# One-bank PSUM tiles in rotation for the up-projection, two weight blocks loaded into other buffers, and a last product added onto sums kept in PSUM

## The chip, the core and the metric

The kernel runs on one core of one Trainium2 chip. The metric is the device time of one execution in microseconds (us), the median of three runs. A core has five engines that run at the same time and meet only through semaphores: TensorE (PE) for matmuls, with its weight loads shown apart as PEld; VectorE (DVE) and ScalarE (ACT) for element-wise work; GpSimd (POOL), used here for tiny operations and a few DMA issues; and SyncE (SP), whose queue issues nearly all DMAs in order. Matmuls write to PSUM, which has 8 banks of 512 fp32 columns each; everything else lives in SBUF.

## The reference

The block mixes 1024 tokens of width 1024, normalises, applies a gated MLP with a causal convolution, and normalises again. What matters here is the second half:

```python
h = layer_norm(ALPHA * h + mix, ln1_g, ln1_b)
u = h @ w_up                                   # 1024 -> 2 x 2816
uc = conv_b + sum(conv_w[j] * pad(u)[:, j:j + T] for j in range(3))
a, v = split(uc, 2)
h = layer_norm(ALPHA * h + (gelu(a) * v) @ w_down, ln2_g, ln2_b)
```

## The kernel before

Every fp32 product is made of three matmuls (`mm3`, lines 83 to 86): each operand is split into a high part `wh` (ACT, line 66) and a low part `wl` (DVE, line 67), and high-high, high-low and low-high are summed in PSUM. One matmul has 128 x 128 weights and 512 moving columns. The order of instructions within each engine's queue is made by a scheduler when the kernel is built: it follows the order of the code where it can and takes later work forward where an instruction would have to wait. A wait at run time therefore stops its engine, and what stands behind it in that queue.

**Up-projection (lines 655 to 687 and 760 to 761).** A seven-product scheme (instead of eight) on 512 x 512 blocks computes, for each of 22 steps `f`, one gate tile and one value tile. `pair(f)` runs seven products of 12 matmuls each (84 in all) into four accumulators c1 to c4. In order: "11" into c1, "12" into c2, "s2" onto c1, "s1" into c3, "s3" onto c1, "s4" onto c3, "22" into c4. Between them ACT and DVE read the accumulators out: line 665 (c1), 669 (c2), 672 (c1), 677 (c3), 680 (c1), 684 (c3), 687 (c4). c1 and c2 are the two halves of one two-bank tile `u`, c3 and c4 of another; the pool `psp` has four such tiles (`unit()`, line 55). Beside it `post(f-1)` runs convolution, GELU and gate (lines 691 to 731), stores the gated blocks to DRAM (`gd`, line 700), and `prep(f+1)` splits the next weights. The weight `s1` of steps from 2 on sits in the pool `lnp` under the tags "g" and "b" in turn (line 640).

**Down-projection (lines 766 to 986).** Again seven products, P1 to P7, each over six blocks `q` of the inner dimension (`plan`, 42 blocks, n = 0 to 41). For each block `load_a` fetches the gated data (line 776) into one of three `rawp` buffers, `prepare` splits data and weight, and `multiply` runs them into four one-bank accumulators per product (`banks`, pool `pb`, opened when `psp` is closed, line 861). A block is 24 matmuls (4 accumulators x 2 inner tiles x 3), the sixth of each product half of that. Splits go into `wp` buffers or, for the operands numbered 5 to 7 modulo 8, into the pool `dn` (tags dh and dl), which is laid over space that the up-projection has given up. The weights of P1's first four blocks come by `load_b` (line 782): blocks 0 and 1 into `rawp`, blocks 2 and 3 into the `tmp` tiles of pool `zq`, which lie over space given up as well. The other weights are loaded in halves by `load_w2` (line 886), two after each `prepare`. The rows of the first norm's scale and offset are loaded into the tags "g" and "b" (line 878, through line 459) before the down-projection starts.

`finish` adds a product's accumulators to the result tiles `z` (lines 910 and 913). P1, P6, P7 and P4 use the first four banks, P2, P5 and P3 the other four. Tiles z[4..7] get in their low half first `ALPHA * b1 - c` after P7, then the scaled residual (`residual`, line 893), then P4's sums (line 913); then their second statistics (line 488) and the norm (lines 470 to 485). In P4 the first two accumulators run through all blocks, then the third, then the fourth, each followed by its `finish` and norm.

Of the kernel before, what the change touches and what calls it, by code (L numbers as in the profile page):

```python
# [9 lines left out]
F32 = mybir.dt.float32  # L10
# [4 lines left out]
ALU = mybir.AluOpType  # L15
AX = mybir.AxisListType

P = 128
T = 1024
D = 1024  # L20
# [7 lines left out]
ALPHA = 2.0 ** 0.25  # L28
# [14 lines left out]
def block_kernel(ctx: ExitStack, tc: tile.TileContext, x, xT, w_ct, w_i, pool_w, w_out, w_up, w_down, pk, rows, masks, ident, out):  # L43
# [11 lines left out]
    def unit():  # L55
        return ps.tile([P, 1024], F32, tag="u", name="u")
# [398 lines left out]
    z = {}  # L455

    def row(i, tag):
        r = lnp.tile([P, D], F32, tag=tag, name=f"row{i}")
        nc.sync.dma_start(out=r, in_=rows[i:i + 1, :].broadcast_to([P, D]))
        return r  # L460
# [4 lines left out]
        G.tensor_tensor(out=rs, in0=rs, in1=epst[:, 0:1], op=ALU.pow)  # L465
        return rs

    def layer_norm(zt, gam, bet, st6, how, sink):
        mv = small.tile([P, 2], F32, tag="mv", name="mv")
        V.bn_aggr(out=mv, in_=st6.rearrange("p a b -> p (a b)"))  # L470
        rs = rstd(mv)
        if how == "added":
            V.scalar_tensor_tensor(out=zt, in0=zt, scalar=mv[:, 0:1], in1=gam, op0=ALU.subtract, op1=ALU.mult)
            A.activation(out=zt, in_=zt, func=AF.Identity, scale=rs)
            G.dma_start(out=zt, in_=rows[3:4, :].broadcast_to([P, D]), accum_op=ALU.add)
            nc.sync.dma_start(out=sink, in_=zt)
            return
        parts = halves if how == "halves" else [slice(0, D)]
        for c in parts:
            V.scalar_tensor_tensor(out=zt[:, c], in0=zt[:, c], scalar=mv[:, 0:1], in1=gam[:, c], op0=ALU.subtract, op1=ALU.mult)  # L480
        if how == "halves":
            parts = [halves[0], slice(512, 768), slice(768, 1024)]
        for c in parts:
            V.scalar_tensor_tensor(out=zt[:, c], in0=zt[:, c], scalar=rs, in1=bet[:, c], op0=ALU.mult, op1=ALU.add)
            nc.sync.dma_start(out=sink[:, c], in_=zt[:, c])

    def stats(zt, c, st6):
        V.bn_stats(out=st6[:, c.start // 512, :], in_=zt[:, c])
# [163 lines left out]
    B11, T1, B21, B22 = block(0, 0), block(0, 1), block(1, 0), block(1, 1)  # L652
    T2, T3, T4 = [[e[:, i] for e in (th, tlo)] for i in range(3)]

    def pair(f):
        w = ops[f]
        u = unit()
        c1, c2 = u[:, lo], u[:, hi]
        prod(c1, w["11"], B11, True, False)
        if f == BRIDGE:  # L660
            yield
            prod(c2, w["12"], B21, True, True)
            yield
        a, v = outs[f] = [ua.tile([P, T], F32, tag=f"u{n}", name=f"u{n}") for n in "av"]
        A.activation(out=a[:, lo], in_=c1, func=AF.Copy)  # L665
        if f != BRIDGE:
            yield
            prod(c2, w["12"], B21, True, True)
        V.tensor_tensor(out=a[:, lo], in0=c2, in1=a[:, lo], op=ALU.add)
        yield  # L670
        prod(c1, w["s2"], T2, False, False)
        A.activation(out=a[:, hi], in_=c1, func=AF.Copy)
        yield
        u = unit()
        c3, c4 = u[:, lo], u[:, hi]
        prod(c3, w["s1"], T1, True, False)
        A.activation(out=v[:, hi], in_=c3, func=AF.Copy)
        yield
        prod(c1, w["s3"], T3, False, True)
        A.activation(out=v[:, lo], in_=c1, func=AF.Copy)  # L680
        V.scalar_tensor_tensor(out=v[:, hi], in0=v[:, hi], scalar=-1.0, in1=v[:, lo], op0=ALU.mult, op1=ALU.subtract)
        yield
        prod(c3, w["s4"], B22, False, True)
        V.tensor_tensor(out=a[:, hi], in0=c3, in1=a[:, hi], op=ALU.add)  # L684
        yield
        prod(c4, w["22"], T4, True, True)
        V.tensor_tensor(out=v[:, lo], in0=c4, in1=v[:, lo], op=ALU.subtract)  # L687
# [46 lines left out]
    def step(gens, n=1):  # L734
        for i in range(n):
            for g in gens:
                next(g, None)
# [21 lines left out]
    step([preps[2]])  # L759
    for f in range(2, NF - 1):  # L760
        step([pairs[2] if f == 2 else pair(f), post(f - 1), preps[f + 1]], 7)

# [15 lines left out]
    raw_b = {}  # L780

    def load_b(q):
        r = rawp.tile([P, 2, 512], F32, tag="raw", name="rawb") if q < 2 else tmp_tile("rawb").rearrange("p (a t) -> p a t", t=512)
        raw_b[q] = r[:, :len(jps[q])]
        nc.sync.dma_start(out=raw_b[q], in_=w_view(0, q, lo))

# [50 lines left out]
    def first_operands():  # L837
        load_a(0)
        load_b(0)
        yield  # L840
        yield
        yield
        prepare(0)
        yield
        load_a(1)
        load_b(1)
        yield
        yield
        load_a(2)
# [5 lines left out]
    tpp.__exit__(None, None, None)  # L855
    bigp.__exit__(None, None, None)
    uap.__exit__(None, None, None)
    psp.__exit__(None, None, None)
    dn = ctx.enter_context(tc.tile_pool(name="dn", bufs=3, reuse_waits="tile"))
    zq = ctx.enter_context(tc.tile_pool(name="zq", bufs=1, reuse_waits="tile"))  # L860
    pb = ctx.enter_context(tc.tile_pool(name="pb", bufs=1, space=bass.MemoryType.PSUM))
    place = {}

    def w_tile(r_, q):
# [2 lines left out]
    def tmp_tile(name):  # L867
        return zq.tile([P, D], F32, tag="tmp", name=name, bufs=3)
# [6 lines left out]
    for q in range(4, NS):  # L875
        w_tile(1, q)
    ww = [[place[r_, q] for q in range(NS)] for r_ in range(2)]
    g1, b1_ = row(0, "g"), row(1, "b")
    st6 = maskt[:, 0, :NC * 48].bitcast(F32).rearrange("p (t a b) -> p t a b", a=2, b=6)

    w_loads = [(0, q, lo) for q in range(FREE, NS)] + [(1, q, lo) for q in range(2)] + [(0, q, c) for q in range(2) for c in (lo, hi)]
# [7 lines left out]
    def residual(t):  # L889
        zn = tmp_tile("zn")  # L890
        nc.sync.dma_start(out=zn, in_=zd[t])
        V.scalar_tensor_tensor(out=zn, in0=zn, scalar=ALPHA, in1=g1, op0=ALU.mult, op1=ALU.mult)
        V.tensor_tensor(out=z[t], in0=z[t], in1=zn, op=ALU.add)

    banks = {i: [pb.tile([P, 512], F32, name=f"c{i}{p}") for p in range(4)] for i in (1, 3)}
    fresh = {P1: 1, P2: 3, P5: 3, P4: 1}
    where = {P1: 1, P6: 1, P7: 1, P4: 1, P2: 3, P5: 3, P3: 3}

    def multiply(n, ps_):
# [6 lines left out]
                mm3(o, ah[:, jj, ts], al[:, jj, ts], wh[:, jj], wl[:, jj], i in fresh and q == 0 and jj == 0,  # L906
                    q == NS - 1 and jj == len(jps[q]) - 1, skip_group_check=True)

    def first_touch(t, c, src, op):
        V.scalar_tensor_tensor(out=z[t][:, c], in0=b1_[:, c], scalar=ALPHA, in1=src, op0=ALU.mult, op1=op)  # L910

    def more(t, c, src, op):
        V.tensor_tensor(out=z[t][:, c], in0=z[t][:, c], in1=src, op=op)

    def finish(i, p):
        c = banks[where[i]][p]
        if i == P1:
            first_touch(p, lo, c, ALU.add)
        elif i == P2:
            more(p, lo, c, ALU.add)  # L920
        elif i == P6:
            first_touch(p, hi, c, ALU.add)
        elif i == P5:
            first_touch(4 + p, hi, c, ALU.subtract)
        elif i == P7:
            more(4 + p, hi, c, ALU.subtract)
            first_touch(4 + p, lo, c, ALU.subtract)
        elif i == P3:
            more(p, hi, c, ALU.add)
        else:  # L930
            more(4 + p, lo, c, ALU.add)

    def norm2(t, c, how):
        stats(z[t], c, st6[:, t])
        layer_norm(z[t], g2, b2, st6[:, t], how, out[t * P:(t + 1) * P, :])


    beside = []
    prepared = 1
    load_b(2)  # L940
    load_b(3)

    def advance(n):
        nonlocal prepared
        while prepared <= n and prepared < len(plan):
            if prepared not in raw_a:
                load_a(prepared)
            prepare(prepared)
            prepared += 1
            if prepared < len(plan) and prepared not in raw_a:  # L950
                load_a(prepared)
            load_w2(2)

    for n in range(6 * NS):
        i, q = plan[n]
        advance(n + 1)
        multiply(n, range(4))
        if q == NS - 1:
            for p in range(4):
                finish(i, p)  # L960
            if i == P6:
                beside += [lambda t=t: (residual(t), stats(z[t], lo, st6[:, t])) for t in range(4)]
            elif i == P7:
                beside += [lambda t=t: (residual(t), stats(z[t], hi, st6[:, t])) for t in range(4, 8)]
        elif beside:
            beside.pop(0)()
            if i == P3 and not beside:
                g2, b2 = row(2, "g"), row(3, "b")
    n0 = 6 * NS
    for q in range(NS):  # L970
        advance(n0 + q + 1)
        multiply(n0 + q, (0, 1))
        if q < 4:
            norm2(q, hi, "added")
    for p in range(2):
        finish(P4, p)
    for q in range(NS):
        multiply(n0 + q, (2,))
    for p in range(2):
        norm2(4 + p, lo, "whole")  # L980
    finish(P4, 2)
    for q in range(NS):
        multiply(n0 + q, (3,))
    norm2(6, lo, "whole")
    finish(P4, 3)
    norm2(7, lo, "halves")


def _consts():
# [60 lines left out]
```

## Time and profile before

| | us |
|---|---|
| median of 3 runs | 1044.73 (1043.55 to 1045.59) |
| the profiled execution | 1043.8 |
| its span in the trace | 1041.9 |
| PE busy | 1022.6 (98%) |
| DVE busy | 814.6 (78%) |
| ACT busy | 446.1 (43%) |

The page gives each engine's busy time as a share of the span and cuts the span into 40 slices of 26 us. A busy PE counts a matmul from start to modelled end (0.39 us), though the next one starts 0.23 us after it, so short waits between matmuls don't lower the busy share: they are to be looked for in the distance between starts and in the waits of the weight loads. The trace answers with a timeline (start, duration, engine, line, operation, output <- inputs, and in brackets the idle time before and who ended it), with waits by who was waited for, and with busy times for stretches.

### The profile page before, as it was taken

The page shows a single profiled execution, that of the slowest core. Times are in us where ns is not written, and L with a number is a line of the kernel's source. Part 1 is how long each engine was busy: PE and PEld are TensorE (multiplying, and loading weights), DVE is VectorE, ACT ScalarE, POOL GpSimd, SP SyncE. Part 2 cuts the span into 40 slices and gives each one's busy share as a digit, 9 for nine tenths or more (in the row PEclk, how much of TensorE's full clock was granted, in tenths as well). Part 3 has the DMA queues.
Part 4 walks back from the last instruction along what each step waited for, and adds up shares of the span by engine and source line. Part 5 has one row for each costly group of instructions (what it writes and reads, how often), then busy time and mean ns, then how long its engine had stood idle before and what let it go on. Part 6 is the DMA issues. An engine that isn't in the chain of part 4 may idle for free.

```text
span 1041.9 us, 12036 instructions
## 1 busy us (share of the span) xinstructions
PE 1022.6 (98%) x4680; PEld 837.6 (80%) x4680; DVE 814.6 (78%) x975; ACT 446.1 (43%) x562; POOL 49.2 (5%) x77
## 2 busy tenths in 40 slices
PE   9999999999999999999999999999999799999996
PEld 6888888888888887878887787787787588888885
DVE  6495488977754779989788888888886669996786
ACT  6421353323631566644444444444454344334340
POOL 2000000001100100000000000000000100000024
PEclk9999999999999999999999999999999999999999
DMA  8200201100142222314314314313315595553347
GB/s 328 91 21 1 81 22 60 41 1 2 60 182 100 99 85 81 112 71 147 105 51 139 115 54 137 113 59 133 112 60 189 200 391 210 172 171 100 122 114 220
DMA packets 42569, 118.63 MB, mean 114 GB/s; under 512 B 4432, under 2 KB 5328, under 8 KB 42512
## 3 DMA queue, kind: packets, MB, share of 16 engines
q1 hardware_dynamic: 41232, 113.86, 31.2%
q0 software_dynamic: 1136, 3.93, 1.5%
q8 instruction: 37, 0.61, 0.2%
q14 instruction: 20, 0.16, 0.0%
q10 hardware_dynamic: 144, 0.07, 0.0%
HBM read 89.27 MB, written 28.57 MB: 113 GB/s over the span
## 4 chain that ended last, share of the span: by engine, by line
PE 96%; DVE 1%; DMA 1%; ACT 0%; issue 0%; SPq 0%; POOLq 0%; POOL 0%; DVEq 0%; ACTq 0%
PE u L84 24%; PE u L86 23%; PE u L85 23%; PE c L85 6%; PE c L84 6%; PE c L86 6%; PE u L229 3%; PE u L269 1%; PE u L530 1%; DMA rawb<-in_w_down 1%; PE u L271 1%; PE u L258 1%; DMA hg<-in_xT 1%; PE u L196 0%; PE u L197 0%
## 5 line engine op out<-in xcount | busy, mean ns | idle before, releaser
L84 PE MATMUL u<-bh,wh 128*128 128x512 f32 x520 | 203.6, 395 | 1.3 <-ACT ua L665 0.7
L85 PE MATMUL u<-bl,wh 128*128 128x512 f32 x520 | 202.8, 390 | 1.0 <-DVE bl L67 1.0
L86 PE MATMUL u<-bh,wl 128*128 128x512 f32 x520 | 202.5, 390 | 0.0
L67 DVE TENSOR_TENSOR wl<-raw,wh 128x1024 fp32r<-128x1024 f32 x85 | 103.4, 1221 | 26.4 <-ACT wh L66 24.0
L66 ACT ACTIVATE wh<-raw 128x1024 fp32r<-128x1024 f32 x85 | 88.9, 1058 | 77.8 <-PE u L85 63.9
L84 PEld LDWEIGHTS u<-bh,wh 128*128 128x128 f32 x520 | 97.6, 188 | 25.2 <-ACT ua L665 3.3
L85 PEld LDWEIGHTS u<-bl,wh 128*128 128x128 f32 x520 | 97.7, 188 | 21.2 <-DVE bl L67 1.6
L86 PEld LDWEIGHTS u<-bh,wl 128*128 128x128 f32 x520 | 97.6, 188 | 21.0
L84 PE MATMUL u<-th,wh 128*128 128x512 f32 x264 | 106.6, 404 | 0.8 <-DVE ua L684 0.8
L86 PE MATMUL u<-th,wl 128*128 128x512 f32 x264 | 103.4, 392 | 0.0
L85 PE MATMUL u<-tlo,wh 128*128 128x512 f32 x264 | 103.1, 391 | 0.0
L84 PEld LDWEIGHTS u<-th,wh 128*128 128x128 f32 x264 | 49.5, 187 | 21.1 <-DVE ua L684 6.9
L66 ACT ACTIVATE wh<-rawa 128x1024 fp32r<-128x1024 f32 (+1 forms) x30 | 30.1, 1002 | 75.0 <-PE c L85 46.5
L86 PEld LDWEIGHTS u<-th,wl 128*128 128x128 f32 x264 | 49.6, 188 | 11.5 <-DVE wl L67 0.3
L693 DVE SCALAR_TENSOR_TENSOR cv<-uv,pkt,cv 128x1023 f32<-128x1023 f32 (+1 forms) x44 | 56.3, 1280 | 2.7 <-ACT cv L691 2.4
L84 PE MATMUL u<-wh,bh 128*128 128x512 f32 x144 | 57.8, 401 | 0.0
L84 PE MATMUL c<-wh 128*128 128x512 f32 x144 | 56.1, 390 | 1.6 <-DVE uv L687 1.6
L85 PEld LDWEIGHTS u<-tlo,wh 128*128 128x128 f32 x264 | 49.6, 188 | 9.1
L693 DVE SCALAR_TENSOR_TENSOR ca<-ua,pkt,ca 128x1023 f32<-128x1023 f32 (+1 forms) x44 | 56.2, 1278 | 0.2
L86 PE MATMUL u<-wh,bl 128*128 128x512 f32 x144 | 56.2, 390 | 0.0
L85 PE MATMUL u<-wl,bh 128*128 128x512 f32 x144 | 56.1, 390 | 0.0
L85 PE MATMUL c<-wl,wh 128*128 128x512 f32 x144 | 56.0, 389 | 0.0
(229 smaller groups left out, 1977.0 us busy)
## 6 DMA issues: line engine op xcount, KB each, us to landing
raw<-in_w_up SPq DMA_DIRECT2D x42, 512.0 KB, 3.5
w<-in_w_down SPq DMA_DIRECT2D x20, 512.0 KB, 10.4
rawa<-gds SPq DMA_DIRECT2D x20, 512.0 KB, 3.5
gd<-ca SPq DMA_DIRECT2D x30, 256.0 KB, 2.9
rawa<-gd SPq DMA_DIRECT2D x15, 512.0 KB, 4.2
raw<-in_w_ct SPq DMA_DIRECT2D x13, 512.0 KB, 3.3
gds<-sm SPq DMA_DIRECT2D x20, 256.0 KB, 2.4
gds<-ca SPq DMA_DIRECT2D x20, 256.0 KB, 4.0
```

The costliest lines, as they stand in the source:

```text
L66: A.activation(out=h, in_=r, func=AF.Copy)
L67: V.tensor_tensor(out=l, in0=r, in1=h.bitcast(F32), op=ALU.subtract)
L84: PE.matmul(o, lhsT=ah, rhs=bh, start=start, stop=False, **kw)
L85: PE.matmul(o, lhsT=ah, rhs=bl, start=False, stop=False, **kw)
L86: PE.matmul(o, lhsT=al, rhs=bh, start=False, stop=stop, **kw)
L229: PE.matmul(ul[:, p * P:(p + 1) * P], lhsT=km[:, p * P:(p + 1) * P], rhs=view(QF, p * P + hh, [2 * hh, 64 // hh], [512 - hh, 2], [1, hh]), ...
L258: PE.matmul(up[:, c * P:(c + 1) * P], lhsT=KTr[:, c * P:(c + 1) * P], rhs=vchunk(c, hs), start=True, stop=True)
L269: PE.matmul(uo[:, cs], lhsT=vchunk(c, hs), rhs=sc[:, cs], start=True, stop=c == 0)
L271: PE.matmul(uo[:, cs], lhsT=S[:, (c - 1) * P:c * P], rhs=QF[:, cs], start=False, stop=True)
L530: PE.transpose(out=ut[:, k * P:(k + 1) * P], in_=z[t][:, k * P:(k + 1) * P], identity=identt)
L693: V.scalar_tensor_tensor(out=c[:, 2 - j:], in0=u[:, :T - 2 + j], scalar=pkt[:, cw + j:cw + j + 1], in1=c[:, 2 - j:], op0=ALU.mult, op1=ALU ...
```

## The change

- `pair` takes its accumulators from `two()`: from step 3 on, two tiles of one bank each from a pool `pb` of eight one-bank buffers in rotation, opened after step 2 when `psp` is closed. The down-projection's eight accumulators are the next eight tiles of the same rotation.
- `load_b` puts weight blocks 2 and 3 into the tags "g" and "b" of `lnp` instead of `tmp` tiles, and both loads are issued within `first_operands`, beside the last `pair`. The rows of the first norm are loaded into these tags later, at n = 3.
- For z[4..7] the low half is no longer collected in `z`. After P7 `ALPHA * b1 - c` is written back into the bank, the residual is added there, and P4's matmuls add onto it. Statistics and the norm's first operation read the bank; P4's four additions are gone. The norm's first operation runs on two halves, the high one first.

```diff
-    def layer_norm(zt, gam, bet, st6, how, sink):
+    def layer_norm(zt, src, gam, bet, st6, how, sink):
...
-        parts = halves if how == "halves" else [slice(0, D)]
-        for c in parts:
-            V.scalar_tensor_tensor(out=zt[:, c], in0=zt[:, c], scalar=mv[:, 0:1], in1=gam[:, c], op0=ALU.subtract, op1=ALU.mult)
-        if how == "halves":
-            parts = [halves[0], slice(512, 768), slice(768, 1024)]
+        for o, c in zip(src, halves[::-1]):
+            V.scalar_tensor_tensor(out=zt[:, c], in0=o, scalar=mv[:, 0:1], in1=gam[:, c], op0=ALU.subtract, op1=ALU.mult)
+        parts = [halves[1], slice(0, 256), slice(256, 512)] if how == "halves" else [whole]
...
+    def two():
+        if f_banks:
+            return [f_banks[0].tile([P, 512], F32, tag="c", name="c") for i in range(2)]
+        u = unit()
+        return u[:, lo], u[:, hi]
...
-        u = unit()
-        c1, c2 = u[:, lo], u[:, hi]
+        c1, c2 = two()
...
-        u = unit()
-        c3, c4 = u[:, lo], u[:, hi]
+        c3, c4 = two()
...
         step([pairs[2] if f == 2 else pair(f), post(f - 1), preps[f + 1]], 7)
+        if f == 2:
+            psp.__exit__(None, None, None)
+            f_banks.append(ctx.enter_context(tc.tile_pool(name="pb", bufs=8, space=bass.MemoryType.PSUM, reuse_waits="tile")))
...
-        r = rawp.tile([P, 2, 512], F32, tag="raw", name="rawb") if q < 2 else tmp_tile("rawb").rearrange("p (a t) -> p a t", t=512)
+        r = (rawp if q < 2 else lnp).tile([P, 2, 512], F32, tag=("raw", "raw", "g", "b")[q], name="rawb")
...
         load_b(0)
+        load_b(2)
...
         load_b(1)
+        load_b(3)
...
-    psp.__exit__(None, None, None)
-    pb = ctx.enter_context(tc.tile_pool(name="pb", bufs=1, space=bass.MemoryType.PSUM))
...
-    g1, b1_ = row(0, "g"), row(1, "b")
...
-        V.tensor_tensor(out=z[t], in0=z[t], in1=zn, op=ALU.add)
+        if t < 4:
+            V.tensor_tensor(out=z[t], in0=z[t], in1=zn, op=ALU.add)
+            return
+        for o, c in ((z[t][:, hi], hi), (banks[1][t - 4], lo)):
+            V.tensor_tensor(out=o, in0=o, in1=zn[:, c], op=ALU.add)
...
-    banks = {i: [pb.tile([P, 512], F32, name=f"c{i}{p}") for p in range(4)] for i in (1, 3)}
-    fresh = {P1: 1, P2: 3, P5: 3, P4: 1}
+    banks = {i: two() + two() for i in (1, 3)}
+    fresh = {P1, P2, P5}
...
-            first_touch(4 + p, lo, c, ALU.subtract)
+            first_touch(4 + p, lo, c, ALU.subtract, c)
...
+            c = banks[1][t - 4]
+            V.bn_stats(out=st6[:, t, 0, :], in_=c)
+            src = [z[t][:, hi], c]
...
-    load_b(2)
-    load_b(3)
...
+        if n == FREE - 1:
+            g1, b1_ = row(0, "g"), row(1, "b")
...
-    for p in range(2):
-        finish(P4, p)
-    for q in range(NS):
-        multiply(n0 + q, (2,))
-    for p in range(2):
-        norm2(4 + p, lo, "whole")
-    finish(P4, 2)
-    for q in range(NS):
-        multiply(n0 + q, (3,))
-    norm2(6, lo, "whole")
-    finish(P4, 3)
-    norm2(7, lo, "halves")
+    for p in range(2, 4):
+        for q in range(NS):
+            multiply(n0 + q, (p,))
+        if p == 2:
+            for t in range(2):
+                norm2(4 + t, "whole")
+    norm2(6, "whole")
+    norm2(7, "halves")
```

## Rows read from the trace of the kernel before

**Rows 1.** The page: the span, and PE's busy tenths in 40 slices.
```profile
span 1041.9 us, 12036 instructions
...
PE   9999999999999999999999999999999799999996
```

**Rows 2.** Stretches (from:to, length, busy us and count of each engine, granted clock, DMA).
```profile
446.53:549.33 102.80, 102.80 (x446) 82.26 (x445) 88.25 (x103) 50.30 (x60) 0.00 (x0) 1.00 0.26 92
549.33:782.67 233.34, 233.34 (x1009) 186.01 (x1009) 197.28 (x229) 109.78 (x132) 0.00 (x0) 1.00 0.30 102
782.67:813.79 31.12, 30.33 (x129) 23.48 (x128) 20.48 (x22) 12.22 (x15) 0.81 (x1) 1.00 0.51 172
...
1014.57:1032.93 18.36, 18.36 (x82) 15.21 (x81) 14.14 (x19) 2.31 (x2) 10.54 (x12) 1.00 0.97 278
```

**Rows 3.** Waits of PE's weight loads, 500 to 809 (us in total, times, longest).
```profile
PEld u L84 <- DVE ua L684: 4.8, 16, 0.3
PEld u L84 <- ACT ua L672: 3.4, 16, 0.4
PEld u L84 <- ACT ua L665: 1.6, 8, 0.2
PEld u L84 <- ACT uv L677: 1.4, 7, 0.2
PEld u L84 <- DVE ua L669: 1.2, 7, 0.2
```

**Rows 4.** Timeline of the last pair: ACT, PE, DVE, PE.
```profile
803.68 0.60 ACT L672 ACTIVATE ua<-u 128x512 f32<-128x512 f32 x1 [3.13 <-PE u L86]
...
809.72 0.39 PE L86 MATMUL u<-bh,wl 128*128 128x512 f32 x1
...
810.14 0.69 DVE L684 TENSOR_TENSOR ua<-u,ua 128x512 f32<-128x512 f32 x1 [1.40 <-PE u L86]
...
810.89 0.50 PE L84 MATMUL u<-th,wh 128*128 128x512 f32 x1 [0.79 <-DVE ua L684]
```

**Rows 5.** Timeline of PE from the last pair to the down-projection's first block.
```profile
813.56 0.39 PE L86 MATMUL u<-th,wl 128*128 128x512 f32 x1
815.50 0.47 PE L84 MATMUL c<-wh 128*128 128x512 f32 x1 [1.55 <-DVE uv L687]
```

**Rows 6.** Timeline before the third block (n = 2): PE, SP's queue, ACT, PE.
```profile
826.26 0.39 PE L86 MATMUL c<-wh,wl 128*128 128x512 f32 x1
...
823.92 0.45 SPq L785 DMA_DIRECT2D rawb<-in_w_down  x1
...
830.64 1.06 ACT L66 ACTIVATE dh<-rawb 128x1024 fp32r<-128x1024 f32 x1 [8.56 <-DMA rawb<-in_w_down]
...
831.75 1.22 PE L84 MATMUL c<-dh,wh 128*128 128x512 f32 x2 [5.10 <-ACT dh L66]
```

**Rows 7.** The third block as a stretch (columns as in rows 2).
```profile
831.75:840.04 8.29, 8.25 (x25) 6.16 (x25) 5.99 (x6) 4.08 (x6) 0.00 (x0) 0.68 1.05 391
```

**Rows 8.** Timeline of SP's queue: the loads into the tags "g" and "b".
```profile
782.00 0.33 SPq L459 DMA_DIRECT2D row<-in_rows  x1
...
804.36 0.33 SPq L459 DMA_DIRECT2D row<-in_rows  x1
```

**Rows 9.** Timeline of DVE: the last post's end, and the third block's low part.
```profile
823.44 0.68 DVE L731 TENSOR_TENSOR ca<-sm,ca 128x512 f32<-128x512 f32 x1
831.73 1.23 DVE L67 TENSOR_TENSOR dl<-rawb,dh 128x1024 fp32r<-128x1024 f32 x1 [7.60 <-ACT dh L66]
```

**Rows 10.** Block n = 7: ACT's split, PE's first matmul, and the stretch around them.
```profile
847.23 1.06 ACT L66 ACTIVATE dh<-rawa 128x1024 fp32r<-128x1024 f32 x1 [5.20 <-DMA rawa<-gd]
...
859.08 0.39 PE L84 MATMUL c<-dh 128*128 128x512 f32 x1
...
845.00:855.00 10.00, 10.00 (x46) 8.26 (x44) 5.16 (x7) 4.02 (x4) 0.00 (x0) 1.00 1.04 394
```

**Rows 11.** Timeline of the end: DVE's addition of P4's last sums.
```profile
1033.36 0.69 DVE L913 TENSOR_TENSOR z<-z,c 128x512 f32<-128x512 f32 x1 [2.08 <-PE c L86]
```

More of the change, by code (lines that the diff above doesn't have):

```diff
@@ L653, in block_kernel @@
     T2, T3, T4 = [[e[:, i] for e in (th, tlo)] for i in range(3)]
+    def two():
[3 more added lines that the diff above has]
+        return u[:, lo], u[:, hi]
+    f_banks = []
     def pair(f):
         w = ops[f]
-        u = unit()
-        c1, c2 = u[:, lo], u[:, hi]
+        c1, c2 = two()
         prod(c1, w["11"], B11, True, False)
@@ L907, in multiply, with first_touch @@
                     q == NS - 1 and jj == len(jps[q]) - 1, skip_group_check=True)
-    def first_touch(t, c, src, op):
-        V.scalar_tensor_tensor(out=z[t][:, c], in0=b1_[:, c], scalar=ALPHA, in1=src, op0=ALU.mult, op1=op)
+    def first_touch(t, c, src, op, o=None):
+        V.scalar_tensor_tensor(out=z[t][:, c] if o is None else o, in0=b1_[:, c], scalar=ALPHA, in1=src, op0=ALU.mult, op1=op)
     def more(t, c, src, op):
@@ L926, in finish, with norm2 @@
             more(4 + p, hi, c, ALU.subtract)
-            first_touch(4 + p, lo, c, ALU.subtract)
+            first_touch(4 + p, lo, c, ALU.subtract, c)
         elif i == P3:
             more(p, hi, c, ALU.add)
-        else:
[L931 to L935, printed above, removed]
+    def norm2(t, how):
+        if t < 4:
+            stats(z[t], hi, st6[:, t])
+            src = z[t]
+        else:
+            c = banks[1][t - 4]
+            V.bn_stats(out=st6[:, t, 0, :], in_=c)
+            src = [z[t][:, hi], c]
+        layer_norm(z[t], src, g2, b2, st6[:, t], how, out[t * P:(t + 1) * P, :])
     beside = []
     prepared = 1
-    load_b(2)
-    load_b(3)
     def advance(n):
@@ L973, in block_kernel @@
         if q < 4:
-            norm2(q, hi, "added")
-    for p in range(2):
-        finish(P4, p)
-    for q in range(NS):
-        multiply(n0 + q, (2,))
-    for p in range(2):
-        norm2(4 + p, lo, "whole")
-    finish(P4, 2)
-    for q in range(NS):
-        multiply(n0 + q, (3,))
-    norm2(6, lo, "whole")
-    finish(P4, 3)
-    norm2(7, lo, "halves")
+            norm2(q, "added")
+    for p in range(2, 4):
[6 more added lines that the diff above has]
+    norm2(7, "halves")
 def _consts():
```

## The prediction

> **What bounds the kernel.** The page comes first: PE is busy in nearly every slice, and only two of the forty show less than nine tenths, the 32nd (807 to 834 us) and the last [rows 1]. So time can be won only where PE waits: in those two slices, and in waits too short for the slices to show. For the short ones I need the ideal pace. Near the end 81 matmul starts take 18.36 us without a wait [rows 2], 0.2267 us each. A pair of the up-projection has 84 matmuls, so 19.04 us. Twelve pairs ran from 549.33 to 782.67, 233.34 us, against 12 x 19.04 = 228.5: 4.8 us lost, 0.40 a pair. The stretch before (446 matmuls, 101.1 us by the pace, 102.80 measured) loses 1.7, the one behind (129 matmuls, 29.2 by the pace, 31.12 measured) 1.9 [rows 2]. Together 8.4 us, some 0.2 us more or less for each record the trace may miss. Third, the waits of the weight loads name the cause, and the timeline shows the three large stops at 810, 814 and 827 us [rows 3 to 6].
>
> **A. One-bank tiles in the pairs.** Of the 54 waits in 500 to 809 us, 31 (L684, L665, L669; 7.6 of 12.4 us) end with a read of the other half of the two-bank tile that PE is about to write: c3 read, c4 wanted; c1 read, c2 wanted; c2 read, c1 wanted [rows 3]. Rows 4 show the largest: "s4" ends, DVE reads c3 for 0.69 us, and only then "22" starts in the other bank, 1.17 us after the matmul before it instead of 0.23. With a tile for each bank this dependency is gone. The other 23 (L672, L677; 4.8 us) are true ones: a product is added onto the bank that ACT has just read. In the code's order 12 matmuls into another accumulator, 12 x 0.2267 = 2.7 us, stand between, and the read takes 0.60 us once ACT gets to it [rows 4]; they are exposed before because parts of "s1" had been taken forward to fill the first kind of wait. Where these fillers are no longer needed, the true waits are covered as well. Bounds: 8.4 x 7.6 / 12.4 = 5.1 us if they stay as they are, 8.4 if all go. I take 7.5, near the upper end, because of the 2.7 against 0.60. The rotation itself costs nothing: a bank comes round again after a whole pair, 19 us after its last matmul, and each is read out within a pair. DVE is busy 197.28 of 233.34 us there [rows 2]; with 12 pairs in 228.5 us it would be at 86%, so it doesn't take over.
>
> **B. The change of stage.** The first block of the down-projection starts 1.94 us after the last pair's last matmul, 1.71 more than the pace; PE waited for L687, the last read of the old pool [rows 5]. The eight accumulators are now the next of the same rotation: 19 pairs (steps 3 to 21) take 76 tiles, so P1's four are the banks of pair 20, long read out, and its operands don't hang on the pool. 1.7 us go, and nothing else is late there; what hides the last read is the first block itself.
>
> **C. The third weight block.** PE stops at 826.26 + 0.23 = 826.49 and goes on at 831.75: 5.3 us [rows 6]. The load was issued at 823.92 on SP's queue and landed 6.7 us later, when ACT started at once. Then the block takes 8.29 us at a granted clock of 0.68 of full speed, against 24 x 0.2267 = 5.4: another 2.85 us [rows 7]. Together 8.1. In the changed kernel blocks 2 and 3 are loaded when "g" and "b" become free. In the trace before, the row loads went into these tags at 782.00 and 804.36 us [rows 8]; so both blocks land some 15 us before they are wanted. What is late next is DVE. Its chain through the last post begins with L684 at 810.14, when "s4" has ended, and runs with hardly a gap to 823.44 + 0.68 = 824.12 [rows 4, 9]; it hangs on "s4", not on PE's waits behind it. PE, without the stops at 810 and 814, would come to block 2 at about 810.0 + 2.7 + 48 x 0.2267 = 823.6. If block 2's low part (1.23 us) stands behind the post on DVE, it is ready at 825.3: 1.7 us are left of the stop. If it is put in front of part of the post: none. If ACT's split can't start before the post has freed its `dn` buffer, which the trace doesn't show: 824.1 + 1.06 + 1.23 = 826.4, 2.8 us. I take the middle, 1.7, because the queue there is full by the rows. A stop of that size before 815.50 left the pace whole (47 starts in the 10.76 us from there to 826.26, 0.229 each [rows 5, 6]), so the 2.85 goes too. C = 8.1 - 1.7 = 6.4, bounds 5.3 and 8.1.
>
> The two row loads that give way (line 878) now stand on SP's queue at n = 3, each behind the split that frees its tag (about 825 and 829). Behind them wait gated data and weights for later blocks. Bytes are the same: two blocks leave the burst, two rows enter it.
>
> **E. What the earlier PE meets.** From 825 us on the DMA queues are full: 394 GB/s at a share of 1.04 from 845 to 855 [rows 10]. The next data to be late is that of block n = 7: ACT got it at 847.23, having waited 5.2 us, so with 1.06 and 1.23 us of splits it is ready at 849.5; PE wanted it at 859.08 [rows 10]. PE comes about 0.9 + 1.7 + 6.4 = 9.0 us earlier after this change: 850.1. So the 9.6 us of cushion are used up, and that is all. If the burst starts as early as before, nothing is lost; for each us that it starts later PE loses one, and 2.85 more should the clock fall. I take 0.5 us lost, bounds 0 and 7 (4 us of stop, the wait for "b", and a fall of the clock).
>
> **D. The end.** After PE's last matmul DVE's addition of 0.69 us stands on the path to the end [rows 11]. It goes. Statistics and the first norm operation now read PSUM. The trace has the same price for both: L913 with one PSUM operand takes 0.69 us, L731 from SBUF alone 0.68 [rows 9, 11]. The four residual additions are split into two of 0.69 each, on a DVE that PE isn't waiting for there, and stand beside P3's first blocks, so P4, which now needs them, finds them done. The two-part norm of tiles 4 to 6 costs DVE about 0.2 us each, inside the 2.08 us that DVE idles before L913 [rows 11]. D = 0.7.
>
> On D the Trainium skill says otherwise: "VectorE: DVE Perf Modes", section "The TRN2 errata — SBUF-src ops pay a fixed extra latency per instruction", gives VectorE a fixed part of 120 cycles from PSUM and 58 from SBUF at 0.96 GHz. By that, two such operations on the last path would cost an estimated 0.13 us more, and D would be 0.6; the rows of this trace show no such difference.
>
> **Sum.** 7.5 + 1.7 + 6.4 + 0.7 - 0.5 = 15.8 us. The profiled execution took 1043.8 us (span 1041.9 and 1.9 around it), which gives 1028.0. The median of the runs is 0.9 above the profiled one, so 1029.
>
> **The rivals.** (1) *The load burst becomes the bound.* For it: the full DMA queues and a cushion of 9.6 us of which 9.0 are used [rows 10]; the row loads wait on the same queue as the burst. Against: two blocks leave the burst, and it waited for no PE. It gives back up to 7 us: 1035 to 1036. (2) *The order of PE's queue leaves waits in the pairs*, at weights or at the true reads: A falls to 3 or so, 1033. For it: 39% of the waits are true ones [rows 3]. (3) *The change doesn't do what it says at block 2*: the load is early, but something else behind the last post frees block 2, or SP's order still puts the loads behind a blocked one. Then C brings nothing: 1035. (4) *Slower: the clock falls in the pairs.* Place: the change from one bank to the next; price: 2.85 us for each fall [rows 7]; it decides from 15.8 / 2.85, six falls in the 19 pairs. One in each pair would give 1029 + 54 = 1083. Against: the granted clock is 1.00 throughout the pairs before, with 54 short waits in it [rows 2, 3], and the change takes waits away.
>
> For rival 4 a page of the Trainium skill speaks: "TensorE: Matmul & The Clock Gate", section "A second HAM failure mode: psum-queue depth-cycling", tells of a kernel that cycled through PSUM banks and whose PE idled briefly between groups so often that the clock swung between its two levels. This trace has cycled through four two-bank tiles with the clock at its higher level, so it doesn't bear that out.
>
> **How the numbers follow.** Forecast, 1024 to 1033: 0.68. Rival 1: 0.13. Rival 2 below what the forecast's range holds: 0.05. Rival 3: 0.05. Rivals 1 and 3 together, or the like, which leaves about no gain: 0.03. Rival 4 and late loads beyond all bounds, slower: 0.06. All gains at their upper ends give 1044.7 - 8.4 - 1.7 - 8.1 - 0.7 = 1025.8; I put the low end at 1024 for records missed in A. All at their lower ends give 1044.7 - 5.1 - 1.7 - 5.3 - 0.6 + 7 = 1039; 8 in 10 are held by 1024 to 1037. About 0.2% (2 us) is what a measurement of this kernel can tell from no change. Faster 0.91, same 0.03, slower 0.06.
>
> **What would show it.** A: the weight loads' waits on L684, L665 and L669 gone, pairs 38.1 us for two instead of 38.9. B: the first c matmul 0.23 us after the last of the pairs. C: `rawb` loaded into the "g" and "b" tiles before 810 us, block 2 started with less than 2 us of stop, granted clock 1.00 around it. E: no PE stop from 840 to 870. D: statistics directly behind the last matmul. Wrong would make it: new waits of PE on weights in the pairs, SP's queue blocked at a row load while the DMA queues run dry, or a granted clock below 1.00 before 800 us.

## The result, and the profile after

The changed kernel takes 1029.66 us (median of 4 runs, 1028.29 to 1031.09) against 1044.33 (4 runs, 1043.55 to 1045.59): a ratio of 0.9859, 95% interval 0.9839 to 0.9878. Forecast were 1029.0 us, range 1024 to 1037. The profiled execution took 1028.29 us with a span of 1026.5, so the spans differ by 1041.9 - 1026.5 = 15.4 us. That is the sum to be explained, against 15.8 forecast.

The page of the kernel after: span, PE's busy tenths in 40 slices and its granted clock.

```profile
span 1026.5 us, 12046 instructions
PE   8999999999999999999999999999999999999997
PEclk9999999999999999999999999999999999999999
```

The weak 32nd slice of before [rows 1] is gone. The slices hide one small stop, which the windows of the kernel after show in the last of three stretches, as 12.42 us busy of 14.00 (us, then busy time and instructions of PE, PEld, DVE, ACT and POOL, granted clock, DMA share, GB/s):

```profile
442.70:800.00 357.30, 357.30 (x1576) 295.43 (x1575) 304.48 (x351) 175.22 (x205) 0.81 (x1) 1.00 0.32 108
800.00:826.00 26.00, 26.00 (x117) 21.52 (x116) 17.30 (x18) 9.80 (x10) 3.24 (x6) 1.00 0.58 180
826.00:840.00 14.00, 12.42 (x54) 9.63 (x53) 9.43 (x11) 5.89 (x7) 0.00 (x0) 1.00 1.05 395
```

The whole list of waits of PE's weight loads from 443 us to 1019 us has two entries, where before had five rows in the pairs alone [rows 3]:

```profile
PEld c L84 <- ACT wh L66: 1.9, 1, 1.9
PEld c L85 <- DVE wl L67: 0.5, 1, 0.5
```

And the timeline of PE at the places where the prediction put its steps (start, duration, engine, line, operation; in brackets idle time and releaser):

```profile
435.38 0.50 PE L84 MATMUL u<-th,wh 128*128 128x512 f32 x1 [0.46 <-ACT ua L677]
...
440.74 0.39 PE L86 MATMUL u<-bh,wl 128*128 128x512 f32 x1
442.01 0.50 PE L84 MATMUL u<-th,wh 128*128 128x512 f32 x1 [0.88 <-DVE ua L688]
...
444.88 0.39 PE L84 MATMUL c<-bh,wh 128*128 128x512 f32 x1
...
806.92 0.39 PE L86 MATMUL c<-th,wl 128*128 128x512 f32 x1
807.15 0.39 PE L84 MATMUL c<-wh 128*128 128x512 f32 x1
...
818.03 0.39 PE L84 MATMUL c<-dh,wh 128*128 128x512 f32 x1
...
828.68 0.39 PE L86 MATMUL c<-dh,dl 128*128 128x512 f32 x1
830.59 1.19 PE L84 MATMUL c<-wh 128*128 128x512 f32 x4 [1.52 <-ACT wh L66]
831.85 0.50 PE L85 MATMUL c<-wl,wh 128*128 128x512 f32 x1
```

From 444.88, where the first one-bank tile is written, to 807.15 the 19 pairs take 362.27 us, which is 1596 matmuls of 0.227: the ideal pace. Two stops are left in the last pair that has two-bank tiles: 0.62 us before 435.38 (L677, L672 before, a true wait) and 1.04 us before 442.01 (the neighbouring half); the second kind stood at 810.89 before [rows 4]. The stage changes within 0.23 us (806.92, 807.15; 1.94 before, [rows 5]). Block 2 starts at 818.03 = 807.15 + 48 x 0.2267 without any stop (5.3 us before, [rows 6]), and the granted clock, 0.68 there before [rows 7], is 1.00. New is the stop at block 4: 828.68 to 830.59, 1.68 us more than the pace, and some 0.5 us behind it where low parts come one by one.

Measured in the two profiled executions: pairs 813.56 - 806.92 = 6.64; stage change 1.71; block 2 with its clock 8.1; block 4 -2.2; the end 1.02. The sum is 15.3.

### The profile page after: what moved, and what is told of

Same layout as the page of the kernel before. It is cut to its first block, busy times and chain, and to the rows that moved or that the text cites. A ratio compares the mean times of both kernels' runs of the same rounds, so it can differ in the third digit from the quotient of the medians.

```text
span 1026.5 us, 12046 instructions
## 1 busy us (share of the span) xinstructions
PE 1012.7 (99%) x4680; PEld 840.6 (82%) x4680; DVE 810.5 (79%) x978; ACT 449.7 (44%) x562; POOL 45.8 (4%) x77
## 4 chain that ended last, share of the span: by engine, by line
PE 92%; DVE 5%; DMA 1%; issue 1%; ACT 1%; SPq 0%; POOL 0%; POOLq 0%; DVEq 0%; ACTq 0%
PE c L85 18%; PE c L86 18%; PE c L84 18%; PE u L84 11%; PE u L85 11%; PE u L86 11%; PE u L229 3%; DVE wl L67 1%; DMA w<-in_w_down 1%; DVE ca L697 1%; DVE cv L697 1%; PE u L269 1%; PE u L528 1%; PE u L271 1%; PE u L258 1%
## 5 line engine op out<-in xcount | busy, mean ns | idle before, releaser
L84 PE MATMUL u<-bh,wh 128*128 128x512 f32 x292 | 115.0, 396 | 1.3 <-ACT ua L670 0.7
L85 PE MATMUL u<-bl,wh 128*128 128x512 f32 x292 | 114.0, 390 | 1.0 <-DVE bl L67 1.0
L86 PE MATMUL u<-bh,wl 128*128 128x512 f32 x292 | 113.8, 390 | 0.0
L84 PE MATMUL c<-bh,wh 128*128 128x512 f32 x228 | 88.7, 389 | 0.0
L85 PE MATMUL c<-bl,wh 128*128 128x512 f32 x228 | 88.7, 389 | 0.0
L86 PE MATMUL c<-bh,wl 128*128 128x512 f32 x228 | 88.7, 389 | 0.0
L84 PE MATMUL c<-th,wh 128*128 128x512 f32 x228 | 88.7, 389 | 0.0
L85 PE MATMUL c<-tlo,wh 128*128 128x512 f32 x228 | 88.7, 389 | 0.0
L86 PE MATMUL c<-th,wl 128*128 128x512 f32 x228 | 88.7, 389 | 0.0
L85 PEld LDWEIGHTS u<-bl,wh 128*128 128x128 f32 x292 | 54.9, 188 | 12.3 <-DVE bl L67 1.6
L697 DVE SCALAR_TENSOR_TENSOR ca<-ua,pkt,ca 128x1023 f32<-128x1023 f32 (+1 forms) x44 | 56.2, 1278 | 0.1
L697 DVE SCALAR_TENSOR_TENSOR cv<-uv,pkt,cv 128x1023 f32<-128x1023 f32 (+1 forms) x44 | 56.2, 1277 | 0.0
```

Of the source, the lines that this page charges most:

```text
L84: PE.matmul(o, lhsT=ah, rhs=bh, start=start, stop=False, **kw)
L85: PE.matmul(o, lhsT=ah, rhs=bl, start=False, stop=False, **kw)
L86: PE.matmul(o, lhsT=al, rhs=bh, start=False, stop=stop, **kw)
L697: V.scalar_tensor_tensor(out=c[:, 2 - j:], in0=u[:, :T - 2 + j], scalar=pkt[:, cw + j:cw + j + 1], in1=c[:, 2 - j:], op0=ALU.mult, op1=ALU ...
```

## The experiments

The times of the runs below stand beside a median of before of 1044.84 us (7 runs, first four experiments) and 1044.31 us (11 runs, last four). The changed kernel ran beside the last four only (1029.27); the first four are set against its 1029.66 above, beside which before took 1044.33, so half a microsecond between them tells nothing.

**Without part 1.** The pairs and the down-projection get their accumulators as before, parts 2 and 3 stay.

```
-        c1, c2 = two()
+        u = unit()
+        c1, c2 = u[:, lo], u[:, hi]
...
-    banks = {i: two() + two() for i in (1, 3)}
+    banks = {i: [pb.tile([P, 512], F32, name=f"c{i}{p}") for p in range(4)] for i in (1, 3)}
```

> The changed kernel with part 1 undone: two-bank tiles in all pairs, the down-projection's accumulators in a pool of their own opened behind the last pair. Theory (the stretch from the last pairs to the fifth block hangs on DVE's chain and on SP's queue behind it, so a gain before it is partly swallowed): the pairs end 6.6 us later and the first down-projection block another 1.7, but weight block 4 lands at a time that hangs on the end of the last 's4' product, so its stop of about 2 us shrinks to next to nothing; 1029.7 + 8.3 - 2 = 1036.0. Rival (parts add up independently): 1029.7 + 8.3 = 1038.0. Second rival (the one-bank tiles gain nothing beside the earlier loads): 1031.

Measured: 1035.5 us (1034.91 to 1036.1), ratio 0.991 [0.9895, 0.9925]. The waits of the pairs are all back (443 to 1019 us):

```profile
PEld u L84 <- DVE ua L690: 6.7, 19, 1.2
PEld u L84 <- ACT ua L678: 3.8, 18, 0.4
PEld u L84 <- ACT ua L671: 2.0, 10, 0.2
PEld c L84 <- ACT wh L66: 1.8, 1, 1.8
PEld u L84 <- DVE ua L675: 1.6, 8, 0.3
PEld u L84 <- ACT uv L683: 1.4, 7, 0.2
```

The theory had 1036.0, its rival 1038.0. The wait on `wh` here is at the first block, which starts at 815.87, 8.72 us later than in the changed kernel; block 4 has no stop. PE's last matmul comes only 6.63 us later. So part 1 wins 8.7 us up to the first block and block 4 takes 2.1 of them: PE comes there before its data.

**Without part 2.** The third and fourth weight block go where they went before, the row loads too.

```
-        r = (rawp if q < 2 else lnp).tile([P, 2, 512], F32, tag=("raw", "raw", "g", "b")[q], name="rawb")
+        r = rawp.tile([P, 2, 512], F32, tag="raw", name="rawb") if q < 2 else tmp_tile("rawb").rearrange("p (a t) -> p a t", t=512)
...
-        if n == FREE - 1:
-            g1, b1_ = row(0, "g"), row(1, "b")
```

> The changed kernel with part 2 undone: weight blocks 2 and 3 loaded into the old places, the first norm's rows loaded before the down-projection. Theory: the load of block 2 is issued some 14 us after the end of the last 's4' and PE can go on about 21.8 us after it, whatever PE does in between; PE now reaches block 2 at 13.8 us after it, so the stop grows from 5.3 to about 8 us, with a fall of the granted clock behind it again, and the stop at block 4 (2.2 us) is gone: 1029.7 + 8.0 + 2.85 - 2.2 = 1038.4. Rival (parts add up independently): 1029.7 + 8.1 - 2.2 = 1035.6.

Measured: 1032.02 us (1031.62 to 1033.34), ratio 0.9879 [0.9864, 0.9894]. Both expectations missed: I had held the load of block 2 to be a fixed stretch behind the last pair's "s4". The timeline of this kernel shows SP, ACT and PE:

```profile
816.07 0.94 SPq L793 DMA_DIRECT2D rawb<-in_w_down  x2
...
820.89 1.06 ACT L66 ACTIVATE dh<-rawb 128x1024 fp32r<-128x1024 f32 x1 [6.57 <-DMA rawb<-in_w_down]
...
818.50 0.39 PE L86 MATMUL c<-wh,wl 128*128 128x512 f32 x1
822.00 1.22 PE L84 MATMUL c<-dh,wh 128*128 128x512 f32 x2 [3.12 <-ACT dh L66]
```

The load is issued 7.85 us earlier than before the change (823.92, [rows 6]), though the pairs end only 5.9 earlier in this execution (807.62), because the gated-data load in front of it on SP's queue hangs on a split that PE's first block sets free, and the first block now begins 1.7 us nearer to the pairs' end. It also lands after 4.8 us instead of 6.7. The stop is 3.3 us instead of 5.3, then 6 us run at half clock, a granted 0.50 (the 1.2 GHz level):

```profile
822.00:828.00 6.00, 5.96 (x13) 4.28 (x14) 3.57 (x3) 2.15 (x3) 0.00 (x0) 0.50 1.03 394
```

The 6.09 us from 822.00 to 828.09 hold 13 matmul starts, 2.95 us at full clock: 3.1 lost. The stop at block 4 is absent. PE ends block 1 0.7 us later than in the changed kernel (818.50 + 0.23 against 818.03); with that, 0.7 + 3.3 + 3.1 - 2.2 make 4.9 of the 5.0 us between the two profiled spans (1031.5 and 1026.5). The profiled execution is the longest of the four here (1033.34) and the shortest of the four of the changed kernel (1028.29); by the medians part 2 is worth 2.4 us in the company of the others. Undone one by one, the three parts give back about 5.8, 2.4 and 0.2 us of 14.7: stops that follow one another share their cushions, and the parts' worths don't add up.

**Without part 3.** Sums of the last round go to SBUF as before.

```
-    fresh = {P1, P2, P5}
+    fresh = {P1: 1, P2: 3, P5: 3, P4: 1}
...
-            first_touch(4 + p, lo, c, ALU.subtract, c)
+            first_touch(4 + p, lo, c, ALU.subtract)
+        else:
+            more(4 + p, lo, c, ALU.add)
```

> The changed kernel with part 3 undone: P4's sums are added to the result tiles by DVE. Theory: one addition of 0.69 us more behind the last matmul and nothing else on the path, 1029.7 + 0.7 = 1030.4; the distance from the last matmul's start to the span's end goes from 7.95 us to about 8.7. Rival (operands in PSUM cost more than the addition saved, or the four additions and split operations move DVE's other work): no change or slower by up to 0.3 per operation, 1029.4 to 1029.7.

Measured: 1029.88 us (1029.73 to 1032.03), ratio 0.9863 [0.9847, 0.9879]: by time it can't be told from the changed kernel, and so not which of theory (1030.4) and rival (1029.4 to 1029.7) is right. The end of the trace shows the parts. First this kernel, whose last matmul starts at 1019.01 (span 1028.0):

```profile
1019.44 0.69 DVE L921 TENSOR_TENSOR z<-z,c 128x512 f32<-128x512 f32 x1 [2.08 <-PE c L86]
1020.16 0.69 DVE L488 BATCH_NORM_STATS2 maskt<-z 128x6 f32<-128x512 f32 x1
...
1022.04 0.93 POOL L465 TENSOR_TENSOR rs<-rs,epst 128x1 f32<-128x1 f32 x1
...
1023.00 1.54 DVE L484 SCALAR_TENSOR_TENSOR z<-z,rs,row 128x512 f32<-128x512 f32 x3 [0.46 <-POOL rs L465]
```

And the changed kernel, last matmul at 1018.55, span 1026.5:

```profile
1018.98 0.70 DVE L949 BATCH_NORM_STATS2 maskt<-c 128x6 f32<-128x512 f32 x1 [3.70 <-PE c L86]
...
1019.96 0.75 DVE L479 SCALAR_TENSOR_TENSOR z<-z,mv,row 128x512 f32<-128x512 f32 x1
...
1020.62 0.74 DVE L479 SCALAR_TENSOR_TENSOR z<-c,mv,row 128x512 f32<-128x512 f32 x1
1020.86 0.56 POOL L465 TENSOR_TENSOR rs<-rs,epst 128x1 f32<-128x1 f32 x1
1021.46 1.55 DVE L482 SCALAR_TENSOR_TENSOR z<-z,rs,row 128x512 f32<-128x512 f32 x3
```

From the last matmul to the span's end 8.99 against 7.95 us: 1.04. Statistics begin 0.72 earlier (1.15 behind the matmul, now 0.43), and from there DVE's last operation comes 0.36 sooner (2.84, now 2.48), because POOL's `pow` takes 0.56 instead of 0.93.

**Block 4's weights on another queue.** In the changed kernel block 4's load is issued on SP at 820.50. The timeline of DVE, SP and ACT shows what holds it there:

```profile
817.16 1.22 DVE L67 TENSOR_TENSOR dl<-rawb,dh 128x1024 fp32r<-128x1024 f32 x1
818.46 0.33 SPq L459 DMA_DIRECT2D row<-in_rows  x1
...
818.89 1.22 DVE L67 TENSOR_TENSOR wl<-rawa,wh 128x1024 fp32r<-128x1024 f32 x1
820.14 0.32 SPq L784 DMA_DIRECT2D rawa<-gd  x1
820.50 6.72 SPq L893 DMA_DIRECT2D w<-in_w_down  x7
...
829.48 1.06 ACT L66 ACTIVATE wh<-w 128x1024 fp32r<-128x1024 f32 x1 [15.85 <-DMA w<-in_w_down]
```

The row load waits for the split of block 3 to free "b" (817.16 + 1.22 = 818.38), the gated data behind it for a split that ends at 820.11, and the weights, which wait for nothing themselves, for both. They land 9.0 us later, on full queues (395 GB/s at a share of 1.05 from 826 to 840 us, above). The experiment issues the first halves of weight blocks 4 and 5 from ACT's queue:

```
-            nc.sync.dma_start(out=w_block(r_, q, c), in_=w_view(r_, q, c))
+            e = nc.scalar if (r_, c) == (0, lo) and q >= FREE else nc.sync
+            e.dma_start(out=w_block(r_, q, c), in_=w_view(r_, q, c))
```

> The changed kernel with one edit: the first halves of weight blocks 4 and 5 are issued from ACT's queue, in front of ACT's split of block 4, not from SP's queue behind the gated data and the row load. Theory (the stop of PE at block 4 comes from the late issue: SP stands at loads that wait for DVE's splits until 820.1 us): the load is issued near 813.6 us, has landed long before 828 us, the stop of 1.7 us and the half us behind it go, 1029.7 - 2.2 = 1027.5. Rival (the DMA queues are the bound, whatever is issued first): the stop stays or moves to the blocks behind, 1029.0 to 1030.0.

Measured: 1026.73 us (1025.78 to 1027.39), ratio 0.9825 [0.9811, 0.984]; its four runs all lie below every run of the changed kernel. The timeline of ACT:

```profile
812.25 0.91 ACTq L894 DMA_DIRECT2D w<-in_w_down  x2
816.18 1.06 ACT L66 ACTIVATE wh<-w 128x1024 fp32r<-128x1024 f32 x1 [2.87 <-DMA w<-in_w_down]
```

And a window of this kernel:

```profile
800.00:840.00 40.00, 40.00 (x178) 33.12 (x177) 28.82 (x31) 16.04 (x17) 3.24 (x6) 1.00 0.79 274
```

Issued 8.25 us earlier, the data are there 3.9 us later, and PE runs through 800 to 840 us without a gap. So the late place in SP's queue makes the stop, and the DMA engines, which move the same bytes, are no bound on the whole. They have a part in it: had the load issued at 820.50 also landed within 3.9 us, at 824.4, block 4 would have had its data in time.

**Which half shares a tile.** The kernel before, with the two-bank tiles shared out otherwise. Its lines are one more than before up to L673 (L672 before), and one less from L676 (L677) on.

```
-        u = unit()
-        c1, c2 = u[:, lo], u[:, hi]
+        u, u2 = unit(), unit()
+        c1, c3 = u[:, lo], u[:, hi]
+        c2, c4 = u2[:, lo], u2[:, hi]
...
-        u = unit()
-        c3, c4 = u[:, lo], u[:, hi]
```

> The kernel before with one edit: the two-bank tiles stay, four in rotation, but c1 and c3 share one and c2 and c4 the other. Theory (PE's short waits come from the sharing of a tile: a product waits for the last read of the tile, whichever half was read): the waits on L665, L669 and L684 leave the list of the pairs, since c2, c1 and c4 now have another neighbour; instead the products into c3 and c1 wait for the reads of their new neighbour, L672, L677 and L680 (line numbers of the kernel before, here one more up to L671 and one less behind). Three exposed reads a pair as before, so about the old time: 1045, between 1041 and 1050. Rival (the waits come from the change from bank to bank, or from the number of tiles in rotation): the list of waits keeps the reads of c1, c2 and c3 before the products into c2, c1 and c4 as its largest part.

Measured: 1046.86 us (1045.98 to 1048.06), ratio 1.0024 [1.0014, 1.0035]. The weight loads' waits from 446 to 809 us:

```profile
PEld u L84 <- ACT ua L673: 5.2, 19, 0.4
PEld u L84 <- ACT uv L679: 4.2, 19, 0.2
PEld u L84 <- ACT uv L676: 3.6, 18, 0.2
```

These are L672, L680 and L677 of before; L665, L669 and L684 have vanished from the list. L672 and L677 could also be true waits, as before; L680 is new, and the other three are gone. The wait has followed the neighbour in the tile, as the theory said, and two pairs take 38.79 us (470.30 to 509.09, by DVE's last read of a pair) against 38.9 before, 38.13 after. The 2.5 us more in the whole kernel come from elsewhere: other waits of 3.3 and 2.8 us, ahead of the pairs (L521 and L568), since the order of PE's queue came out otherwise there too. With them, and some 5 us at half pace behind them, the last 1596 matmuls of the pairs begin 7.7 us later than before (450.65 against 442.96); they take 367.92 us against 370.60 before and 362.04 after.

**One-bank tiles later.** The changed kernel, with `if f == 12` in place of `if f == 2`.

> The changed kernel, with the pool of one-bank tiles opened behind step 12 instead of step 2. Theory (part 1 is worth 0.40 us for each pair): ten more pairs in two-bank tiles lose 4.0 us: 1033.7, the waits on the reads of a neighbouring half are back up to about 625 us and gone after it, and the stop of about 1 us that stands in the last two-bank pair moves from 442 us to about 630. Rival (the pairs' gain comes once, from the end of the stage, and the short waits are hidden anyway): 1029.7.

Measured: 1033.91 us (1032.3 to 1034.46), ratio 0.9894 [0.9878, 0.9911]: 4.6 us above the changed kernel beside it, 4.0 expected for ten pairs. The list of waits from 443 to 640 us has the old reads, and the larger stop of the last two-bank pair stands at 637; from 640 to 809 us there is no wait.

```profile
PEld u L84 <- DVE ua L688: 4.0, 10, 1.2
PEld u L84 <- ACT ua L677: 1.8, 9, 0.2
PEld u L84 <- ACT uv L681: 1.5, 3, 1.1
...
```

The stop in the timeline of PE:

```profile
637.14 0.50 PE L84 MATMUL u<-th,wh 128*128 128x512 f32 x1 [0.78 <-DVE ua L688]
```

**A rotation of four.** The changed kernel with `bufs=4` for the pairs and a second tag of four for P1's accumulators.

> The changed kernel, with four one-bank tiles in rotation for the pairs and the four others for the first accumulators of the down-projection. Theory (what counts is that each bank is a tile of its own; a bank is read out long before a pair has passed): as the changed kernel, 1029.7, no wait in the pairs. Rival (the depth of eight counts, since four one-bank tiles are half of the PSUM that the pairs had before): waits at the first product of a pair on the reads of the pair before, up to 0.40 us a pair, 1037.

Measured: 1029.6 us (1028.32 to 1030.63), ratio 0.9857 [0.9843, 0.9872], no wait in the pairs. What counts is that a tile is one bank; four in rotation are enough.

**The changed kernel beside them.**

> The changed kernel itself, beside the three others on the same chip: 1029.7, between 1028.3 and 1031.1. Both theories expect the same; it is the base for the differences to the others.

Measured: 1029.27 us (1027.83 to 1030.47), ratio 0.9854 [0.9839, 0.9869].

## Why the prediction was right, point by point

- **A, 7.5 (bounds 5.1 to 8.4): 6.64 measured.** Mechanism right, and shown: the waits follow the tile's neighbour when the halves are exchanged, come back for ten pairs when the pool is opened later, and need no rotation of eight. The true waits (L672, L677) vanished as well, as argued. What was mis-sized is a cost that the term put at nothing: pair 2, which the change leaves in two-bank tiles, now has the two stops shown above, 0.62 and 1.04 us. Before, matmuls of the next product had been taken forward into these places (at 434.80 and 441.15). By count, the same matmul begins 0.05 us earlier than before at 433.39 and 1.92 us later at 444.88: 1.97 us are lost in this pair. The 1596 matmuls from there on take 362.04 us from first to last start, 370.60 before (the pace gives 361.6): 8.56 won, a little above the upper bound, so nothing was left to win in these pairs. With the pool opened ten steps later, two such stops stand in the last two-bank pair again, at 628 and 637 us. The new pool also carries an option that the old one lacks (`reuse_waits`), which no run separates; the exchange of the halves, under the old pool, shows that the neighbour decides which waits there are.
- **B, 1.7: 1.71.** Right in size and place.
- **C, 6.4 (bounds 5.3 to 8.1): 8.1.** The step that failed is the residual of 1.7: of the three orders that I priced, DVE took the one with the split of block 2's weights ahead of the post's convolution (L697), so nothing remained of the stop:

```profile
806.64 1.22 DVE L67 TENSOR_TENSOR dl<-rawb,dh 128x1024 fp32r<-128x1024 f32 x1
...
808.37 1.28 DVE L697 SCALAR_TENSOR_TENSOR ca<-ua,pkt,ca 128x1023 f32<-128x1023 f32 x1
```

  That the 2.85 us behind the stop go too was right: the granted clock is 1.00 throughout. Not all of them were the clock's: before, block 2's low part was ready at 831.73 + 1.23 = 832.96 [rows 9], and the first two matmuls and the wait for it took 1.26 us, of which 0.8 would have been lost at full clock too. The worth of part 2 alone is another matter: with part 1 in place, undoing it costs 2.4 us by the medians, since the old load also comes earlier then.
- **E, 0.5 lost at block 7 (bounds 0 and 7): 2.2 lost at block 4.** The step that failed is "the next data to be late is that of block n = 7". Block 7's cushion of 9.6 us was rightly read, and block 4's was about the same: before, ACT began its weights at 834.41, so they were ready at 835.47, and PE was there at 845.48, 10.0 us. What decided is how far each load came forward. Two rows of before, and below the dots two of the kernel after:

```profile
834.41 1.06 ACT L66 ACTIVATE wh<-w 128x1024 fp32r<-128x1024 f32 x1 [0.36 <-DMA w<-in_w_down]
845.48 0.39 PE L84 MATMUL c<-wh 128*128 128x512 f32 x1
...
833.38 1.04 ACT L66 ACTIVATE dh<-rawa 128x1024 fp32r<-128x1024 f32 x1
844.70 0.39 PE L84 MATMUL c<-dh 128*128 128x512 f32 x1
```

  Block 7's split now begins at 833.38, 13.9 us earlier (847.23, [rows 10]), and PE wants it at 844.70, 14.4 us earlier (859.08): 9.1 us of the cushion are left. At block 4 PE would have come 16.6 us earlier (828.91), its load was issued 4.5 us earlier (824.99, now 820.50) and the data came 4.9 us earlier: 10.0 + 4.9 - 16.6 = -1.7, the stop. Counted as in the prediction, from the end of "s4" (its read began 5.5 us earlier, 804.63 for 810.14), PE gained 11.1 us and not 9.0, most of it because C gave all its 8.1, and the weights lost 0.6: 11.1 + 0.6 - 10.0 = 1.7. The queue behind the row loads was named, but not followed to the block that needs it first, and the stretch that the prediction watched, 840 to 870 us, begins behind the stop. The ACT-queue run shows the cause.
- **D, 0.7: 1.02.** The addition's 0.72 as forecast; the other 0.3 is POOL's `pow`, which I did not price. Statistics from PSUM take 0.70 us, those from SBUF 0.69, and the norm's halves 0.74 and 0.75: the dearer PSUM operand of the Trainium skill ("VectorE: DVE Perf Modes", section "The TRN2 errata — SBUF-src ops pay a fixed extra latency per instruction") is not seen here.
- **Rivals.** The load burst as the bound (1) fell with the ACT-queue run, though full queues lengthen the one late load; PE's order left no waits (2); part 2 does what it says (3); and the clock never fell in the pairs (4), with eight one-bank tiles in rotation or with four, so what the Trainium skill tells of in "TensorE: Matmul & The Clock Gate", section "A second HAM failure mode: psum-queue depth-cycling", does not appear.

That the forecast of 1029.0 met 1029.66 so closely is luck: A and E gave 2.6 us less than their terms, C and D 2.0 us more.

## What to carry to other kernels

A tile of two banks makes a product into one bank wait for a read of the other: some 0.4 us a pair here, spread over waits that no slice of the page shows, and found by counting matmuls against the ideal pace. The banks themselves can be used side by side: with a tile for each, PE wrote one while another was read (DVE's read of c3 at 804.63, PE without a wait from 444.88 to 828.68), and lost nothing. When stops are removed, look through every load behind them for its cushion, the time from landing to use, less what PE gains and plus what the load gains; the smallest that is left decides, not the smallest of before: here 9.6 us held and 10.0 did not. And a load that waits for nothing may stand in an in-order queue behind two that wait for buffers: another queue was worth 2 to 3 us here, for two lines.

## What the runs showed of the hardware

- **The clock behind a stop.** Behind the stops of 1.68 and 1.88 us at block 4 (two profiled executions of the changed kernel) the granted clock stayed at 1.00, and PE was back at 0.23 us a matmul from 832.42 and 833.58 on, with the seventh; behind 1.80 and 1.79 us (without part 3, and the rotation of four) it stayed at 1.00 too. Behind one of 1.96 us (one-bank tiles later) the granted clock was 0.54 from 835.36 to 839.00, with five matmuls 0.43 us apart, 1.7 us lost; behind 3.3 us (without part 2) it was 0.50 for 6 us, 3.1 us lost; behind 5.3 us 2.85 us were lost [rows 7]. In the last two, 0.8 us of the loss was the wait for a low part. So a stop can cost nearly its own length again, and the longest here did not cost the most.
- **POOL beside DVE.** The same `pow` on 128x1 takes 0.92 or 0.93 us at the end when DVE runs `z<-z,mv,row` beside it, with all inputs in SBUF, and 0.56 or 0.57 us when DVE's operation takes `c` from PSUM or DVE is idle. The Trainium skill, "SBUF — State Buffer", section "SBUF: two separate sides", says that a DVE operation with two SBUF inputs and a GpSimd operation that reads SBUF hold the port pair that they share in turn, each for the whole instruction; the rows agree: in both kernels that have SBUF inputs there, before and without part 3, `pow` ends 0.41 and 0.43 us behind the end of DVE's operation. POOL's spans are rough, but these repeat. Moving one input to PSUM so gave POOL 0.36 us on the path to the end.
